# Attention layer: token reordering in two halves, weight splits in another place of the plan, another order of the first loads and projections

## The chip, the cores and the metric

One core of a Trainium2 chip runs the whole program. The metric is the device time of one execution in microseconds (us). The core's engines work side by side, each through its own queue of instructions in a fixed order: TensorE (PE: matmuls and transposes), VectorE (DVE), ScalarE (ACT), GpSimd (POOL), and SyncE (SP), which here only issues the DMA transfers. An instruction that waits holds what stands behind it on its engine.

## The reference

One decoder layer in float32 on x of 1 x 1024 x 1024 (sequence 1024, width 1024): RMS norm, dilated sliding-window attention, added to x; RMS norm, a gated FFN with a short convolution, added to x. Cut to the part that the change touches:

```python
ATTN_GROUPS = ((128, 1), (512, 4), (2048, 16))      # (window, dilation)

def dilated_attention_mixer(h, w_in, q_gain, k_gain, w_out):
    B, S, _ = h.shape
    proj = (h @ w_in).reshape(B, S, 3, 3, 8, 64)      # group, (q, k, v), head, head dim
    outs, lses = [], []
    for g, (window, dilation) in enumerate(ATTN_GROUPS):
        q = rms_norm(proj[:, :, g, 0], q_gain[g]) * 64 ** -0.5
        k = rms_norm(proj[:, :, g, 1], k_gain[g])
        o, lse = dilated_window_attention(q, k, proj[:, :, g, 2], window, dilation)
        outs.append(o); lses.append(lse)
    weights = softmax(stack(lses), axis=0)
    o = sum(weights[..., None] * stack(outs), axis=0)
    return o.reshape(B, S, 512) @ w_out

x = x + dilated_attention_mixer(rms_norm(x, mixer_norm), ...)
x = x + conv_ffn(rms_norm(x, ffn_norm), ...)
```

## The kernel before

**Precision.** Every operand of a matmul is kept as a rounded high part and a low part, the rest. A product is three matmuls: high by high, high by low, low by high. So a weight tile that has arrived is split: ACT casts its high part (L179), and DVE or POOL subtracts to get the low part (L180; DVE for k tiles 0, 2, 4, 5, 7, POOL for 1, 3, 6). Tokens are split in the same way after the transposes that follow the norm (L113; high L115 on ACT, low L116 on DVE) into `hh` and `hl`, which hold the normed x transposed, in eight k tiles of 128 x 1024 with one slot to spare, nine in all.

**Units and blocks.** The attention is done in six units u: the groups in the order 2, 2, 1, 1, 0, 0, each in two halves of four heads. A unit is eight blocks of 128 tokens, 48 blocks in all. Block i projects its tokens (`project`, L198 to L200, into `qk`, and `project_v`, L207 to L209, into `vp`, over eight k tiles each), and then, while PE already projects block i+1, passes through these steps: `norm` (square on ACT, `ss` on DVE, then `ms` and `rs` on POOL, L79 and L80), `values` (`v`, ACT then DVE, L227 and L228), `kept` (POOL makes a part of `kT`), `scale` (`qn`, DVE, L220), `heads_T` (PE transposes to `tr`, L256), `heads_split` (`qT`, `kT`, ACT and DVE), `scores` (`s`, PE, L285), `softmax` (`ust` on DVE, L311; `sm` on ACT, L314), `weights_T` and `weights_split` twice (`pt` on PE, L322; `pT` on ACT and DVE), `attend` twice (`u`, PE), `finish` (DVE, L347) and a write of the block's result to `ud` on SP.

**Weights.** A unit's eight weight tiles are loaded by SP into `raw` (three buffers), split by `load_w` into `w`, a ring of WA = 11. So tiles 0 to 2 of a unit are split far ahead, 3 to 7 in the block before the unit begins, as the old unit's tiles come free.

**Token order.** Each group wants the tokens in another order. Between group 2 and 1 (block 15) and 1 and 0 (block 31) `reorder(g, k)` copies k tile k of `hh` (DVE for even k, ACT for odd) and of `hl` (POOL) into the slot that is free, in the new order; that slot's predecessor becomes free for the next k. A copy of one k is two instructions for g = 1 (L135), four for g = 0 (L142). A copy for k can only run after the last block of the old unit has projected the tile that it overwrites.

**What sets the order.** A list `plan` holds every step with a due time (`at(t, f, ...)`), eight units of time to a block; block i projects k at 8i + k, its v at 8i + 2.6 + 0.85k, and its later steps at 8i + 8 plus an offset from the table `T` (val 0.6, scale 2.5, hT 4.2, sc 6.45, sm 6.5, w0 8.3, a0 12.2, fin 14.4). The steps are written in the order of due times, and PE, ACT, DVE and POOL run them in the order written; the order of SP's DMA issues is made by the scheduler of the tile framework from that order and from what each transfer waits for. `make_masks` (due 90) makes two tables of positions, `kpos`, on POOL, transposes them on PE and makes the masks of groups 1 and 0 on DVE. `tp_gains` loads the gains of q and k and transposes them. `wraw` is a tag of four buffers that x tiles, the first raw tiles, `kpos` and the output weights `w_out` use one after another.

## Time and profile before

| | us |
|---|---|
| median of 3 runs (lowest, highest) | 1334.71 (1334.53, 1338.65) |
| the profiled execution, device time | 1336.1 |
| its span in the trace | 1334.2 |
| PE busy | 1284.2 (96%) |
| DVE busy | 901.2 (68%) |
| ACT busy | 616.0 (46%) |
| POOL busy | 495.9 (37%) |

The page of the profile is read from PE, the busiest engine: a view of the waits names, for PE's idle stretches, the instruction that waited and what released it; the timeline shows instructions of an engine one after another with the idle time before each; the view of stretches gives each engine's busy time, and the granted clock of TensorE as a part of full speed, in a stretch of time that one chooses.

### The profile page before, as it was taken

To read this page: it belongs to the slowest core of one execution; us is meant where nothing else is said; L and a number is where in the kernel's file an instruction comes from. 1 tells how busy PE (TensorE), PEld (TensorE's weight loads), DVE (VectorE), ACT (ScalarE), POOL (GpSimd) and SP (SyncE) were. 2 spreads that over 40 slices of the span, in tenths; PEclk is the share of its full clock that TensorE was granted. 3 is DMA by queue.
4 is the path that set the end of the run, shared out by engine and by line. 5 is a ranking of instruction groups with operands and counts; after the bars stand their busy time and mean duration, and the time that the engine had idled before them with its cause. 6 is when DMAs were issued, how large, how long until landed. Compare 5 with 4: busy or idle time off the path is not lost.

```text
span 1334.2 us, 19243 instructions
## 1 busy us (share of the span) xinstructions
PE 1284.2 (96%) x6911; PEld 1078.4 (81%) x6911; DVE 901.2 (68%) x1544; ACT 616.0 (46%) x1277; POOL 495.9 (37%) x599
## 2 busy tenths in 40 slices
PE   6999998999999999999988999999999999999998
PEld 4898887888878888887766788888888887888887
DVE  4665455454564565556776898888888888876664
ACT  4655354444454444435544444444444536444442
POOL 4333345333354555454533554454454443000000
PEclk9999999999998999999999999999999999999999
DMA  7112212112111121113721333323332328973341
GB/s 240 41 64 75 86 37 72 34 48 61 48 46 35 51 58 50 31 39 122 227 77 39 94 104 111 102 82 100 118 115 83 111 71 283 348 250 105 95 143 64
DMA packets 111614, 132.16 MB, mean 99 GB/s; under 512 B 6126, under 2 KB 80030, under 8 KB 111518
## 3 DMA queue, kind: packets, MB, share of 16 engines
q1 hardware_dynamic: 111518, 130.93, 30.7%
q8 instruction: 55, 0.90, 0.3%
q14 instruction: 41, 0.34, 0.1%
HBM read 95.91 MB, written 35.00 MB: 98 GB/s over the span
## 4 chain that ended last, share of the span: by engine, by line
PE 43%; DVE 3%; issue 2%; DMA 1%; POOL 1%; ACT 1%; SPq 0%; DVEq 0%; POOLq 0%; ACTq 0%
PE ua L687 15%; PE y L871 15%; PE uc L687 8%; PE ub L687 4%; DVE c L732 1%; DMA wB<-in_ffn_w_down 1%; POOL wxl L518 0%; DMA graw<-gde 0%; ACT c L730 0%; DVE sz L660 0%; DVE sy L656 0%; DVE c L743 0%; DVE bt L598 0%; POOL wyl L518 0%; POOL wzl L518 0%
## 5 line engine op out<-in xcount | busy, mean ns | idle before, releaser
L871 PE MATMUL y<-wd,g 128*128 128x512 f32 x924 | 210.4, 389 | 0.2
L871 PEld LDWEIGHTS y<-wd,g 128*128 128x128 f32 x924 | 173.4, 188 | 36.9 <-DVE wd L598 0.6
L198 PE MATMUL qk<-w,hh 128*128 128x512 f32 x384 | 159.0, 414 | 0.5 <-ACT hh L115 0.5
L199 PE MATMUL qk<-w,hh 128*128 128x512 f32 x384 | 153.5, 400 | 0.0
L200 PE MATMUL qk<-w,hl 128*128 128x512 f32 x384 | 152.6, 397 | 0.5 <-DVE hl L116 0.5
L79 POOL TENSOR_SCALAR ms<-ss 128x8 f32<-128x8 f32 (+1 forms) x64 | 12.9, 201 | 312.9 <-DVE ss L216 265.9
L207 PE MATMUL vp<-w,hh 128*128 128x256 f32 x384 | 122.8, 320 | 3.6 <-DVE v L228 3.6
L732 DVE SCALAR_TENSOR_TENSOR c<-uu,cw,c 128x1023 f32<-128x1023 f32 (+1 forms) x44 | 95.6, 2174 | 38.3 <-ACT c L730 37.5
L209 PE MATMUL vp<-w,hl 128*128 128x256 f32 x384 | 108.8, 283 | 0.0
L208 PE MATMUL vp<-w,hh 128*128 128x256 f32 x384 | 108.8, 283 | 0.0
L518 POOL TENSOR_TENSOR wyl<-sy,wyh 128x1024 fp32r<-128x1024 f32 x21 | 56.5, 2689 | 115.0 <-issue 61.0
L80 POOL TENSOR_TENSOR rs<-ms,half 128x8 f32<-128x8 f32 (+1 forms) x64 | 87.5, 1367 | 5.4
L207 PEld LDWEIGHTS vp<-w,hh 128*128 128x128 f32 x384 | 73.5, 192 | 18.5 <-DVE v L228 5.8
L314 ACT ACTIVATE sm<-sm,ust 128x128 f32<-128x128 f32 (+1 forms) x128 | 53.4, 418 | 76.0 <-DVE ust L311 73.4
L200 PEld LDWEIGHTS qk<-w,hl 128*128 128x128 f32 x384 | 73.3, 191 | 18.7 <-DVE hl L116 1.2
L267 ACT ACTIVATE qT<-tr,gains 128x256 fp32r<-128x256 f32 x48 | 22.7, 473 | 134.8 <-PE tr L256 134.8
L216 DVE TENSOR_REDUCE ss<-qn 128x8 f32<-128x512 f32 x48 | 32.9, 685 | 75.8 <-ACT qn L214 75.8
L208 PEld LDWEIGHTS vp<-w,hh 128*128 128x128 f32 x384 | 73.6, 192 | 9.3
L270 DVE SCALAR_TENSOR_TENSOR qT<-tr,gains,qT 128x256 fp32r<-128x256 f32 x48 | 23.2, 484 | 85.5 <-ACT kT L269 85.5
L518 POOL TENSOR_TENSOR wxl<-uraw,wxh 128x1024 fp32r<-128x1024 f32 x22 | 58.4, 2653 | 44.8 <-ACT wxh L517 44.7
L198 PEld LDWEIGHTS qk<-w,hh 128*128 128x128 f32 x384 | 74.0, 193 | 1.1 <-ACT hh L115 0.9
L199 PEld LDWEIGHTS qk<-w,hh 128*128 128x128 f32 x384 | 74.1, 193 | 0.1
(186 smaller groups left out, 3363.0 us busy)
## 6 DMA issues: line engine op xcount, KB each, us to landing
uraw<-in_ffn_w_up SPq DMA_DIRECT2D x44, 512.0 KB
raw<-in_attn_w_in SPq DMA_DIRECT2D x48, 384.0 KB
wB<-in_ffn_w_down SPq DMA_DIRECT2D x44, 256.0 KB
graw<-gds SPq DMA_DIRECT2D x44, 256.0 KB
gdo<-c SPq DMA_DIRECT2D x11, 512.0 KB
gds<-gbc SPq DMA_DIRECT2D x11, 512.0 KB
graw<-gdo SPq DMA_DIRECT2D x22, 256.0 KB
ud<-ust SPq DMA_DIRECT2D x32, 132.0 KB
```

The lines of the kernel that those rows point to most:

```text
L80: nc.gpsimd.tensor_tensor(r[:, :n], t[:, :n], half[:, :n], op=ALU.pow)
L198: nc.tensor.matmul(self.qk, a, w[:, 0, :512], start=k == 0, stop=False)
L199: nc.tensor.matmul(self.qk, a, w[:, 1, :512], start=False, stop=False)
L200: nc.tensor.matmul(self.qk, b, w[:, 0, :512], start=False, stop=k == KT - 1)
L207: nc.tensor.matmul(self.vp, a, w[:, 0, 512:], start=k == 0, stop=False)
L208: nc.tensor.matmul(self.vp, a, w[:, 1, 512:], start=False, stop=False)
L209: nc.tensor.matmul(self.vp, b, w[:, 0, 512:], start=False, stop=k == KT - 1)
L314: nc.scalar.activation(sm[:, h, lo:], sm[:, h, lo:], AF.Exp, scale=-1.0, bias=st[:, 256 + h:257 + h], accum_out=st[:, 260 + h:261 + h])
L518: eng.tensor_sub(l, raw, h.bitcast(F32))
L687: nc.tensor.matmul(acc[:, lo:hi], w[z][:, s + k], a[y][:, j, k, lo:hi], start=begin and lo == 0 and k == 0 and n == 0, stop=k == 3 and n == 2,
L732: nc.vector.scalar_tensor_tensor(c[:, k:], u[:, :S - k], cw[:, 2 - k, j:j + 1], c[:, k:], op0=ALU.mult, op1=ALU.add)
L871: nc.tensor.matmul(y, gs[:, z, ts], ws[:, w], start=f and n == 0, stop=k == NK - 1 and n == 2, skip_group_check=True)
```

## The change

Five edits, all in the attention part:

- **The first loads and block 0.** SP issues x of chunk 0, the gain row `gbc`, raw tiles 0 to 4, x of chunk 1, raw tiles 5 to 7; before, raw tile 0 came ahead of `gbc`, and x of chunk 1 behind raw tile 2. DVE scales chunk 0 ahead of the first weight split. Chunk 1 is scaled behind four of DVE's five splits of unit 0, before behind two (counting the one ahead of chunk 0); its transposes were due at 0.5 and 0.6 and are due at 5.5 and 5.7, between the v projections of k tiles 3 and 4 of block 0. The loads of the q and k gains have a step of their own (2.5), and their transposes are due at 8.3.
- **The masks.** POOL's part, `kpos`, becomes `mask_places`, due at 76.8; PE's and DVE's part stays in `make_masks`, due at 86.5.
- **The reordering.** `reorder` takes the half (h or l), the k tile and the copying engine. The low half's k = 0 to 4 are copied by POOL from 28 units ahead of the block before the change of group, one every five units, into `hl`'s free slot and, for group 1, four further tiles `hx` (tag `wraw`); group 0 reads these and writes back to `hl`. The low k = 5 to 7 follow in the block itself. The high half's k = 0 is copied on ACT 4.4 units ahead of that block; k = 1 to 7 follow in it at offsets given by a table, odd k on ACT, even k on DVE.
- **The weight splits.** Tiles 3 to 7 of a new unit were due 3.1 to 7.1 units into the block before it. Now tile 3 is due at 3.9, and 4 to 7 at 8.7, 9.45, 10.6 and 12.6 where u is even, at 5.4, 8.7, 9.6 and 10.8 where u is odd; `values` of that block is at 8.6. The issue of raw tiles 6 and 7 goes with the splits of 3 and 4.
- **What follows for SP.** Since `hx` and the output weights share the tag `wraw`, `w_out`'s loads wait for `hx`'s last readers in block 31; before, they followed `kpos`.

```diff
@@ -117,29 +118,37 @@
 
 
 
-    slot0 = {2: 0, 1: 8, 0: 7}
-
-    def toks(g, t, k, c):
-
-        return t[:, (k + slot0[g]) % (KT + 1), c * P:(c + 1) * P]
-
-    def reorder(g, k):
-
-        for t, copy in ((hh, nc.scalar.copy if k % 2 else nc.vector.tensor_copy), (hl, nc.gpsimd.tensor_copy)):
-            src, dst = (t[:, (k + slot0[x]) % (KT + 1)] for x in (g + 1, g))
-            if g == 1:
-
-                src = src.rearrange("p (e r b n) -> p e r b n", e=2, r=4, b=2)
-                dst = dst.rearrange("p (r b e n) -> p e r b n", e=2, r=4, b=2)
+    places = {("h", 2): [*range(8)], ("h", 1): [8, *range(7)], ("h", 0): [7, 8, *range(6)],
+              ("l", 2): [*range(8)], ("l", 1): [8, "a", "b", "c", "d", 0, 1, 2],
+              ("l", 0): [3, 4, 5, 6, 7, 8, 0, 1]}
+    extra = {}
+
+    def place(z, g, k):
+        s = places[z, g][k]
+        return extra[s] if isinstance(s, str) else (hh if z == "h" else hl)[:, s]
+
+    def toks(g, z, k, c):
+
+        return place(z, g, k)[:, c * P:(c + 1) * P]
+
+    def reorder(g, z, k, copy):
+
+        if isinstance(places[z, g][k], str):
+            extra[places[z, g][k]] = A.tile([P, S], F32R, name="hx", tag="wraw", bufs=4)
+        src, dst = place(z, g + 1, k), place(z, g, k)
+        if g == 1:
+
+            src = src.rearrange("p (e r b n) -> p e r b n", e=2, r=4, b=2)
+            dst = dst.rearrange("p (r b e n) -> p e r b n", e=2, r=4, b=2)
+            for e in range(2):
+                copy(dst[:, e], src[:, e])
+        else:
+
+            src = src.rearrange("p (r b e c n) -> p b c e r n", r=4, b=2, e=2, c=4)
+            dst = dst.rearrange("p (b c e r n) -> p b c e r n", r=4, b=2, e=2, c=4)
+            for b in range(2):
                 for e in range(2):
-                    copy(dst[:, e], src[:, e])
-            else:
-
-                src = src.rearrange("p (r b e c n) -> p b c e r n", r=4, b=2, e=2, c=4)
-                dst = dst.rearrange("p (b c e r n) -> p b c e r n", r=4, b=2, e=2, c=4)
-                for b in range(2):
-                    for e in range(2):
-                        copy(dst[:, b, :, e], src[:, b, :, e])
+                    copy(dst[:, b, :, e], src[:, b, :, e])
 
     def rows(g, t, c):
 
...
@@ -193,7 +202,7 @@
 
             if k == 0:
                 self.qk = PQ.tile([P, 512], F32, name="qk", bufs=2)
-            a, b = toks(self.g, hh, k, self.c), toks(self.g, hl, k, self.c)
+            a, b = toks(self.g, "h", k, self.c), toks(self.g, "l", k, self.c)
             w = Ws[self.u, k]
             nc.tensor.matmul(self.qk, a, w[:, 0, :512], start=k == 0, stop=False)
             nc.tensor.matmul(self.qk, a, w[:, 1, :512], start=False, stop=False)
@@ -202,7 +211,7 @@
         def project_v(self, k):
             if k == 0:
                 self.vp = PA.tile([P, 256], F32, name="vp", bufs=1)
-            a, b = toks(self.g, hh, k, self.c), toks(self.g, hl, k, self.c)
+            a, b = toks(self.g, "h", k, self.c), toks(self.g, "l", k, self.c)
             w = Ws[self.u, k]
             nc.tensor.matmul(self.vp, a, w[:, 0, 512:], start=k == 0, stop=False)
             nc.tensor.matmul(self.vp, a, w[:, 1, 512:], start=False, stop=False)
@@ -409,57 +418,77 @@
     def first(i):
         xs[i] = Normed(i, xs[i])
 
-    def tp_gains():
-        grow = A.tile([P, 4, P], F32, name="grow", tag="qn", bufs=2)[:6, 0]
+    gr = {}
+
+    def load_gains():
+        gr[0] = grow = A.tile([P, 4, P], F32, name="grow", tag="qn", bufs=2)[:6, 0]
         for t in range(2):
             nc.sync.dma_start(grow[0:3, t * DH:(t + 1) * DH], q_gain)
             nc.sync.dma_start(grow[3:6, t * DH:(t + 1) * DH], k_gain)
+
+    def tp_gains():
+        grow = gr[0]
         tp = PA.tile([P, 512], F32, name="tp", tag="tr", bufs=2)
         nc.tensor.transpose(tp[:, :6], grow, ident[:6, :6])
         nc.vector.tensor_scalar(gains[:, 0:3], tp[:, 0:3], DH ** -0.5, None, op0=ALU.mult)
         nc.vector.tensor_copy(gains[:, 3:6], tp[:, 3:6])
 
-    def make_masks():
-        places = A.tile([P, 8, P], F32, name="kpos", tag="wraw", bufs=4)
-        kpos, kint = places[:, 0:2], places[:, 2:4].bitcast(I32)
+    kp = {}
+
+    def mask_places():
+        t = A.tile([P, 8, P], F32, name="kpos", tag="wraw", bufs=4)
+        kp[0] = kpos = t[:, 0:2]
+        kint = t[:, 2:4].bitcast(I32)
         nc.gpsimd.iota(kint[:, 0], pattern=[[1, 8], [8, 16]], base=0, channel_multiplier=0)
         nc.gpsimd.iota(kint[:, 1], pattern=[[1, 2], [2, 64]], base=0, channel_multiplier=0)
         nc.gpsimd.tensor_copy(kpos, kint)
-        kp = PA.tile([P, 4, P], F32, name="kp", tag="tr", bufs=2)
+
+    def make_masks():
+        kpos = kp[0]
+        t = PA.tile([P, 4, P], F32, name="kp", tag="tr", bufs=2)
         for g in range(2):
-            nc.tensor.transpose(kp[:, g], kpos[:, g], ident)
-        nc.vector.tensor_copy(qpos, kp[:, 0:2, 0])
+            nc.tensor.transpose(t[:, g], kpos[:, g], ident)
+        nc.vector.tensor_copy(qpos, t[:, 0:2, 0])
         for g in range(2):
             for j, beyond in enumerate((ALU.is_lt, ALU.is_gt)):
                 nc.vector.tensor_scalar(mask[:, g, j], kpos[:, g], qpos[:, g:g + 1], NEG, op0=beyond,
                                         op1=ALU.mult)
 
     blocks = [Block(u, n) for u in range(6) for n in range(8)]
-    early = [(-20, -19.6, -19.35, -18), (-19.1, -17.8, -17.65, .5)]
+    early = [(-20, -19.2, -19.15, -18.9), (-19.3, -18.4, -18.2, 5.5)]
     for i in range(8):
         t = early[i] if i < 2 else (8 * i - 12, 8 * i + T["xf"], 8 * i + T["xs"], 8 * i + T["xt"])
         at(t[0], get_x, i)
         at(t[1], first, i)
         at(t[2], lambda i: xs[i].scale(), i)
         at(t[3], lambda i: xs[i].turn(0), i)
-        at(t[3] + .1, lambda i: xs[i].turn(1), i)
-    at(-19.4, get_gain)
-    at(2.5, tp_gains)
-    at(90, make_masks)
+        at(t[3] + .2, lambda i: xs[i].turn(1), i)
+    at(-19.9, get_gain)
+    at(2.5, load_gains)
+    at(8.3, tp_gains)
+    at(76.8, mask_places)
+    at(86.5, make_masks)
     for g, i in ((1, 16), (0, 32)):
-        for k in range(KT):
-            at(8 * (i - 1) + T["vs"] * (k - 1) + T["v"] + .02, reorder, g, k)
+        t = 8 * (i - 1)
+        at(t - 4.4, reorder, g, "h", 0, nc.scalar.copy)
+        for k in range(5):
+            at(t - 28 + 5 * k, reorder, g, "l", k, nc.gpsimd.tensor_copy)
+        for k, d in enumerate((2.62, 3.47, 4.6, 5.3, 6.1, 7.3, 8.65), 1):
+            at(t + d, reorder, g, "h", k, nc.scalar.copy if k % 2 else nc.vector.tensor_copy)
+        for k, d in enumerate((3.5, 5.3, 7.0) if g == 1 else (3.5, 7.2, 9), 5):
+            at(t + d, reorder, g, "l", k, nc.gpsimd.tensor_copy)
     SP = WA - KT
     for u in range(6):
         wt = {}
         for kt in range(KT):
             if u == 0:
-                t = lead = (-19.5, -19.3, -19.2)[kt] if kt < 3 else -18 + .1 * kt
+                t = (-19.1, -19, -18.8, -18.6, -18.5, -18.3, -18.1, -18)[kt]
+                lead = -19.8 + .1 * kt if kt < 5 else -18.7 + .05 * kt
             elif kt < SP:
                 t = 64 * u - 32 + T["wp"] + 4 * kt
                 lead = t - 3
             else:
-                t = 64 * u - KT + max((kt - SP) * T["vs"] + T["v"] + .01, kt - SP + T["w"])
+                t = 64 * u - KT + (3.9, *((8.7, 9.45, 10.6, 12.6) if u % 2 == 0 else (5.4, 8.7, 9.6, 10.8)))[kt - SP]
                 lead = max(t - 8, 64 * u - KT + (kt - SP - 3) * 1. + T["w"] + .5) if kt < SP + 3 else wt[kt - 3] + .3
             wt[kt] = t
             at(lead, load_raw, u, kt)
```

What stands on the engines is shown at three places. PE at the start: transposes `xT` of a chunk of x, then block 0's projections (`qk`, `vp`), three matmuls to a k tile. Before, from the first instruction on:

```order
L113 MATMUL xT<-ident,xn 128x128 x8
L198 MATMUL qk<-w,hh 128x512
L199 MATMUL qk<-w,hh 128x512
L200 MATMUL qk<-w,hl 128x512
L113 MATMUL xT<-ident,xn 128x128 x8
L198 MATMUL qk<-w,hh 128x512
L199 MATMUL qk<-w,hh 128x512
L200 MATMUL qk<-w,hl 128x512
```

and now, behind the first transposes, five k tiles of `qk` and three of `vp`:

```order
L207 MATMUL qk<-w,hh 128x512
L208 MATMUL qk<-w,hh 128x512
L209 MATMUL qk<-w,hl 128x512
L216 MATMUL vp<-w,hh 128x256
L217 MATMUL vp<-w,hh 128x256
L218 MATMUL vp<-w,hl 128x256
L114 MATMUL xT<-ident,xn 128x128 x8
L216 MATMUL vp<-w,hh 128x256
L217 MATMUL vp<-w,hh 128x256
L218 MATMUL vp<-w,hl 128x256
L207 MATMUL qk<-w,hh 128x512
```

The second set of transposes stood behind the first k tile of `qk`; now it stands behind six of `qk` and four of `vp`.

DVE in the first part of block 15, the last of group 2 (`qn` from `qk` is the scaling, `hh<-hh` a high copy, `w<-raw` a weight split, `ust<-u` is `finish`). Before:

```order
L329 TENSOR_TENSOR pT<-pt,pT 128x256
L135 COPY hh<-hh 128x8x64 x2
L220 TENSOR_TENSOR qn<-qk,rs 128x512
L135 COPY hh<-hh 128x8x64 x2
L329 TENSOR_TENSOR pT<-pt,pT 128x256
L180 TENSOR_TENSOR w<-raw,w 128x768
L270 SCALAR_TENSOR_TENSOR qT<-tr,gains,qT 128x256
L273 SCALAR_TENSOR_TENSOR kT<-tr,gains,kT 64x2x128 x2
L180 TENSOR_TENSOR w<-raw,w 128x768
L135 COPY hh<-hh 128x8x64 x2
L347 TENSOR_REDUCE ust<-u 128x256
L135 COPY hh<-hh 128x8x64 x2
```

and now:

```order
L338 TENSOR_TENSOR pT<-pt,pT 128x256
L229 TENSOR_TENSOR qn<-qk,rs 128x512
L144 COPY hh<-hh 128x8x64 x2
L338 TENSOR_TENSOR pT<-pt,pT 128x256
L279 SCALAR_TENSOR_TENSOR qT<-tr,gains,qT 128x256
L282 SCALAR_TENSOR_TENSOR kT<-tr,gains,kT 64x2x128 x2
L144 COPY hh<-hh 128x8x64 x2
L356 TENSOR_REDUCE ust<-u 128x256
```

Four copies and two splits stood there, two copies stand there now.

DVE at the end of block 15 (`ss` belongs to `norm`, `v` to `values`). Before:

```order
L180 TENSOR_TENSOR w<-raw,w 128x768
L216 TENSOR_REDUCE ss_2303<-qn 128x8
L228 TENSOR_TENSOR v<-vp,v 128x4x64
L329 TENSOR_TENSOR pT<-pt,pT 128x256
L220 TENSOR_TENSOR qn<-qk,rs 128x512
L329 TENSOR_TENSOR pT<-pt,pT 128x256
L270 SCALAR_TENSOR_TENSOR qT<-tr,gains,qT 128x256
L273 SCALAR_TENSOR_TENSOR kT<-tr,gains,kT 64x2x128 x2
```

and now:

```order
L144 COPY hh<-hh 128x8x64 x2
L225 TENSOR_REDUCE ss_2291<-qn 128x8
L237 TENSOR_TENSOR v<-vp,v 128x4x64
L189 TENSOR_TENSOR w<-raw,w 128x768
L338 TENSOR_TENSOR pT<-pt,pT 128x256
L189 TENSOR_TENSOR w<-raw,w 128x768
L229 TENSOR_TENSOR qn<-qk,rs 128x512
L338 TENSOR_TENSOR pT<-pt,pT 128x256
L279 SCALAR_TENSOR_TENSOR qT<-tr,gains,qT 128x256
L282 SCALAR_TENSOR_TENSOR kT<-tr,gains,kT 64x2x128 x2
L189 TENSOR_TENSOR w<-raw,w 128x768
```

One split stood ahead of `ss`; now one copy stands there, two splits stand between `v` and the scaling, and one behind `kT`.

## Rows read from the trace of the kernel before

**Rows 1.** Page, part 1: busy time, share of the span, instructions.

```profile
PE 1284.2 (96%) x6911; PEld 1078.4 (81%) x6911; DVE 901.2 (68%) x1544; ACT 616.0 (46%) x1277; POOL 495.9 (37%) x599
```

**Rows 2.** PE's waits, 0 to 560 us: total us, times, longest us.

```profile
PE xT L113 <- DVE xn L107: 11.9, 2, 9.0
PE pt L322 <- ACT sm L314: 6.1, 2, 3.1
PE vp L207 <- DVE v L228: 3.6, 5, 1.1
PE kp L430 <- POOL kpos L427: 3.0, 1, 3.0
PE tr L256 <- DVE qn L220: 2.3, 2, 1.8
...
PE qk L198 <- ACT hh L115: 0.5, 1, 0.5
...
PE s L285 <- POOL kT L245: 0.3, 1, 0.3
```

**Rows 3.** Timeline of PE, start: start us, length us, instruction, [idle before <- releaser].

```profile
11.49 0.80 PE L198 MATMUL qk<-w,hh 128*128 128x512 f32 x1 [0.55 <-ACT hh L115]
...
16.90 1.94 PE L113 MATMUL xT<-ident,xn 128*128 128x128 f32 x8 [2.89 <-DVE xn L107]
...
20.77 0.63 PE L200 MATMUL qk<-w,hl 128*128 128x512 f32 x1
...
28.73 0.40 PE L198 MATMUL qk<-w,hh 128*128 128x512 f32 x1
```

**Rows 4.** Timelines of DVE and ACT, start.

```profile
7.64 1.28 DVE L107 SCALAR_TENSOR_TENSOR xn<-xt,rs,gbc 128x1024 f32<-128x1024 f32 x1
...
13.92 2.83 DVE L107 SCALAR_TENSOR_TENSOR xn<-xt,rs,gbc 128x1024 f32<-128x1024 f32 x1 [0.17 <-POOL rs L80]
...
17.00 0.83 ACT L179 CAST w<-raw 128x768 fp32r<-128x768 f32 x1 [0.23 <-DMA raw<-in_attn_w_in]
```

**Rows 5.** Timelines of POOL and DVE about the masks.

```profile
144.50 1.64 POOL L80 TENSOR_TENSOR rs<-ms,half 128x8 f32<-128x8 f32 x1
...
147.81 0.88 DVE L434 TENSOR_SCALAR mask<-kpos,qpos 128x128 f32<-128x128 f32 x4
```

**Rows 6.** Stretches: length; busy PE, PEld, DVE, ACT, POOL; clock, DMA, GB/s.

```profile
148.00:151.40 3.40, 3.40 (x12) 2.93 (x11) 1.62 (x6) 0.13 (x1) 0.12 (x1) 0.50 0.29 89
...
410.80:414.20 3.40, 3.40 (x15) 3.14 (x14) 1.57 (x3) 0.29 (x1) 0.00 (x0) 0.51 0.00 0
```

**Rows 7.** PE's waits, 195 to 215 us (blocks 15 and 16).

```profile
PE pt L322 <- ACT sm L314: 3.1, 1, 3.1
PE s L285 <- DVE kT L273: 1.0, 1, 1.0
PE vp L207 <- DVE v L228: 0.8, 1, 0.8
PE tr L256 <- DVE qn L220: 0.6, 1, 0.6
```

**Rows 8.** Timelines of DVE, POOL and ACT about block 15.

```profile
193.03 0.76 DVE L135 CAST hh<-hh 128x512 fp32r<-128x512 f32 x2
194.57 0.69 DVE L220 TENSOR_TENSOR qn<-qk,rs 128x512 f32<-128x512 f32 x1 [0.78 <-POOL rs L80]
195.18 1.51 DVE L135 CAST hh<-hh 128x512 fp32r<-128x512 f32 x2
...
200.57 0.96 DVE L180 TENSOR_TENSOR w<-raw,w 128x768 fp32r<-128x768 f32 x1
...
213.69 0.69 DVE L220 TENSOR_TENSOR qn<-qk,rs 128x512 f32<-128x512 f32 x1 [2.28 <-POOL rs L80]
...
200.85 5.94 POOL L135 CAST hl<-hl 128x512 fp32r<-128x512 f32 x8
...
203.12 1.14 ACT L135 CAST hh<-hh 128x512 fp32r<-128x512 f32 x2 [3.13 <-DVE hh L135]
```

## The prediction

> **What bounds the kernel now.** I read the page first: TensorE (PE) is busy for 96% of the span [rows 1], so it is the bound, and a change can gain only where PE stands still or runs slowly, or lose by making it stand. Next, PE's waits up to 560 us, in which the whole attention lies [rows 2, 7]: the reader is to see that they add up to some 29 us, and nearly all lie in five kinds of place. At the start PE waits 11.9 us in two goes for the normed x (`xT <- xn`) and 0.5 us each for the first high and the first low part (two rows, one shown). At 147 us it waits 3.0 us for `kpos`, which GpSimd (POOL) makes for the masks. At the five unit ends it waits 3.6 us for `v`. The other waits (`pt <- sm`, `tr <- qn`, `s <- kT`) lie where one token order is turned into the next, in blocks 15 and 31. For the first of these I asked the same view of 195 to 215 us alone [rows 7]: 1.0 + 3.1 + 0.8 + 0.6 = 5.5 us. Third, the granted clock: in four stretches of 3.4 us, at 148, 206, 400.6 and 410.8 us, each just behind such a wait, PE had 0.50 or 0.51 of its clock, so 1.2 instead of 2.4 GHz (the first and the last stand in [rows 6]); at the higher level the work in one would have taken half the time, so each costs 1.7 us. The start has a stretch like it: a 128x512 matmul takes 0.63 us at 20.8 us and 0.40 us at 28.7 us [rows 3].
>
> **Start.** Two edits act. The first split of block 0's weights (0.96 us) no longer runs on VectorE (DVE) ahead of `xn` of chunk 0, which starts at 7.64 us now [rows 4]; it can start at about 6.85, when its row scale is there. That moves the first projection from 11.49 us [rows 3] to about 10.5. The larger: after three matmuls PE now turns to chunk 1's transposes and waits for its `xn`, and block 0's other projections stand behind them. After the change six weight tiles of block 0 come first and the transposes behind v of tile 3. So PE works from 10.5 us on, and the 11.8 us of PE work that lie between the second transposes at 16.9 us and block 1's second projection at 28.73 us [rows 3] follow the first three matmuls (1.3 us): 10.5 + 1.3 + 11.8 = 23.6 us. Half clock is in that figure, since PE runs its first 5 us at it either way. Against it stand arrivals: the last raw tile lands at 17.0 us now [rows 4], and the same bytes are asked for in nearly the same order. ACT's cast (0.83 us) and DVE's split (0.96) follow, and `xn` of chunk 1 stands ahead of that split on DVE: 1.28 us alone, 2.83 beside POOL [rows 4]. So the last low part is there between 19.2 and 20.7 us, with about 2 us of PE work behind it, and block 1's second projection comes between 22.6 and 25.2 us. I take 24.0: a gain of 4.7 us (3.5 to 6.1). The q and k scales' transposes cost their 0.1 us in either place; their loads, issued earlier, have 3 us more to land.
>
> **Masks.** `kpos` was late because its instructions stood behind a 1.64 us `rs` on POOL [rows 5]. They move to a gap of POOL 13 of the plan's units earlier (eight are a block), and PE's two transposes find them ready. That removes 3.0 us and, with the gap, the half clock behind it: 4.7 us. The DVE part (0.88 us for four instructions [rows 5], and a smaller one) now runs in a steady block, ahead of `sm`, where PE has some slack; I charge 0.5. Gain 4.2 us (3.5 to 4.7).
>
> **Waits for v.** Of 3.6 us, 0.8 belong to block 15 [rows 7]. The other 2.8, at the ends of units 0, 2, 4 and in block 31, come from two or three splits of the next unit that stand on ACT and DVE ahead of `v`. At the odd units' starts one of five is left ahead, and the rest goes behind `v`, where one split of 0.96 us fits in DVE's gap. All 2.8 go (1.4 to 2.8).
>
> **Reordering at block 15.** Here DVE did four high copies of 1.5 us beside POOL (0.76 alone), and splits, ahead of `kT`, `sm` and `v`; ACT waited 3.13 us in its row for one of DVE's; POOL copied for 5.94 us in one go, which made `kT`, `ms` and `rs` late [rows 8]. After the change five of eight low copies are done 5 to 28 units earlier, in POOL's idle time; one high copy goes to ACT before the stage; two splits go from before `sm` to behind `v`. That leaves on DVE one copy of 1.5 us in each of three places. The 3.1 us before `pt` go: ahead of `sm` stand one copy and `ust` instead of two copies, `ust`, a split and the waits between. What becomes late next: `tr` of block 15. Between `ss` and the scaling of `qn` DVE has 2.28 us in which it waits for POOL's `rs` [rows 8]. Into it now go two splits. ACT must first do v, a 1.14 us copy and a 0.83 us cast, so that the first split can start some 1.4 us after v; with 0.96 + 0.41 (`pT`) + 0.96 behind it, scaling comes 3.7 us after v, where PE's own work from v to `tr` is 2.7. I charge 1.2 us for it, 1.4 for three short waits (`pt`, `vp`, `u`) behind copies of 1.5 us on DVE and 1.14 on ACT, and 0.3 for a chance of half clock: 2.9 left of 5.5 + 1.7 = 7.2. Gain 4.3 us. The bounds: 7.2 if nothing is late, 2 if the short waits stay as they were.
>
> **Reordering at block 31.** The same sum: by rows 2 less rows 7, 3.0 (`pt`) + 1.7 (`tr`) + 0.3 (`s`) = 5.0 us (its v is counted above), and two half-clock stretches, 3.4: 8.4. Block 31 scores two tiles of keys, so PE has more work of its own between the same steps, and I leave only `tr` behind the two splits, 1.3 us. Gain 7.1 us (5 to 8.4).
>
> **What else moves, at nothing.** The early low copies, ten of about 1.5 us each (5.94 for four [rows 8]), go to POOL, busy for 37% of the span [rows 1]. They lengthen DVE work that runs beside them: the one high copy was 1.51 instead of 0.76 us, but scaling of `qn` beside POOL's copies took its usual 0.69 [rows 8], and most of DVE's work in a steady block is of this kind, reading PSUM. If each of ten cost PE 0.3 us, it would be 3 us; I take zero. On SP, w_out's four loads now need the extra tiles' last reader in block 31 and stand there between two raw tiles of unit 4; the tile behind them is needed by ACT some 6 us after it can land. The raw tile of kt 7 is issued only after kt 4's split; from the start, where eight such tiles and more landed in 17 us [rows 4], I estimate that it lands within some 2 us, about one before it is cast. Cover gone, each microsecond would be one of PE.
>
> By the rows a DVE copy beside POOL costs 1.51 us instead of 0.76 [rows 8], and that is what I used. The Trainium skill (SBUF — State Buffer, section "Who interferes with whom") says more: who issues first has the ports shared by DVE and GpSimd for its whole instruction, and the other is blocked. Before, POOL's copies were short ones; after, one of DVE's copies in block 15 meets POOL's split of a whole weight tile. By that rule it would wait for all of it, an estimated 1 us more in `sm`, and the sum would be 22 instead of 23 us.
>
> **Sum.** 4.7 + 4.2 + 2.8 + 4.3 + 7.1 = 23.1 us. PE's row count is the same, and all behind the attention (out-projection, FFN, down-projection) is untouched and waits for PE, so the gain passes through. The profiled execution took 1336.1 us with a span of 1334.2; less 23.1 that is 1313.0. It lies 1.4 us above the median of the runs, 1334.71, from which 1311.6 follows. I say 1311.5.
>
> **Rivals.** First, *the splits behind v become the new wait*. At the two even boundaries scaling waits longer than I sum, PE stands for 2.5 to 3 us, and the clock halves behind it. For: the row with 2.28 us has no room for two splits and their casts; before, one `tr` wait of 1.7 was followed by half clock [rows 6]. Against: PE's own work covers 2.7 of it. Each place 3 to 4.5 us: 1316 to 1325, likeliest 1319. Second, *all waits go*: copies and splits overlap better than by rows; then 29 us are gained, 1305.5. Third, *slower*: a single mechanism, SP's queue at the even boundaries. SP issues in order; a raw tile that waits for a split which waits for the ring's slot holds w_out and the `ud` writes behind it, and PE waits for weights. It decides from about 3 us later than summed; to be slower than before it has to cost 11.5 us at each of two places beyond that, and over 13 to be measurably so: 1339. Against: the same estimate of 2 us for a landing, and a DMA share of 0.00 in the stretch just behind block 31's waits [rows 6]. Fourth, *it doesn't do what it says*: the order is on the engines, but arrivals set the start and the copies just shift their lateness; within 4 us of before, 1333.
>
> **How the numbers follow.** The forecast 0.63, own range 1306 to 1316; splits as a new wait 0.20; all gone 0.11; slower 0.03; no effect 0.03. The range takes in the forecast, most of the first rival and the edge of the second: 1305.5 to 1320. A measurement here tells about 0.3%, 4 us, from no change. Faster 0.94, same 0.03, slower 0.03.
>
> **What would show it.** Start: block 1's second projection at 24 us, and no `xT` wait but the first, at 8.2. Masks: no `kp` wait, clock 1.00 behind it. v: no `vp` waits at odd units. Boundaries: no `pt` wait over 1 us, a `tr` wait of 1 to 1.5, clock near 1. Wrong would be a `tr`, `s` or `qk` wait of over 2 us there, a second half-clock stretch, or PE waiting for a raw tile.

## The result, and the profile after

The changed kernel takes 1315.38 us (median of four runs, 1313.31 to 1317.68) against 1335.76 for the kernel before on the same chips: a ratio of 0.9845, 95% interval 0.9821 to 0.9869, so 20.4 us less (17.5 to 23.9). The forecast was 1311.5, 23.2 us less than the median of before known then, in a range of 1305.5 to 1320. The profiled execution went from 1336.1 to 1315.75 us, its span from 1334.2 to 1313.7.

PE's waits up to 560 us in the changed kernel, the view of [rows 2, 7] (total us, times, longest us):

```profile
PE xT L114 <- DVE xn L108: 8.6, 2, 8.4
PE tr L265 <- DVE qn L229: 3.0, 5, 0.9
PE qk L208 <- POOL w L189: 0.6, 1, 0.6
PE qk L208 <- DVE w L189: 0.4, 2, 0.3
PE pt L331 <- ACT sm L323: 0.3, 1, 0.3
```

29 us of waiting have become 13. `kp` and both long waits for `sm` are gone, and with them the half clock that followed: the stretches that answer to [rows 6], behind the masks, block 15 and block 31 (two), now run at the full 2.4 GHz (stretch; busy PE, PEld, DVE, ACT, POOL; granted clock; DMA share; GB/s):

```profile
138.00:141.40 3.40, 3.40 (x21) 2.65 (x20) 1.35 (x3) 1.58 (x6) 1.69 (x2) 1.00 0.00 0
...
193.00:196.40 3.40, 3.25 (x18) 2.51 (x18) 1.19 (x4) 3.38 (x11) 1.31 (x2) 1.00 0.00 1
...
382.00:385.40 3.40, 3.40 (x21) 2.75 (x20) 1.52 (x3) 3.38 (x10) 1.86 (x3) 1.00 0.72 280
392.00:395.40 3.40, 3.40 (x28) 2.95 (x25) 2.19 (x10) 2.21 (x9) 0.00 (x0) 1.00 0.50 146
```

Five waits for `qn` stand where there were two, one at each of the five unit changes. One of them, and the start, on PE's timeline (start us, length us, instruction, idle before and its releaser):

```profile
10.43 0.79 PE L207 MATMUL qk<-w,hh 128*128 128x512 f32 x1
11.02 0.63 PE L208 MATMUL qk<-w,hh 128*128 128x512 f32 x1
11.44 0.57 PE L209 MATMUL qk<-w,hl 128*128 128x512 f32 x1
11.86 0.40 PE L207 MATMUL qk<-w,hh 128*128 128x512 f32 x1
...
14.63 0.50 PE L208 MATMUL qk<-w,hh 128*128 128x512 f32 x1 [0.63 <-POOL w L189]
...
18.46 1.06 PE L114 MATMUL xT<-ident,xn 128*128 128x128 f32 x8 [0.19 <-DVE xn L108]
...
23.45 0.40 PE L207 MATMUL qk<-w,hh 128*128 128x512 f32 x1
...
199.07 0.66 PE L265 MATMUL tr<-ident,qn 128*128 128x128 f32 x4 [0.70 <-DVE qn L229]
```

**A ledger by place.** PE runs the same instructions in nearly the same order in both kernels, so the start of the same projection can be read in both timelines and subtracted. Here it is the second projection (k = 1) of a block; a block's row runs from there to the next block's second projection.

| stretch | forecast us | changed kernel us | where |
|---|---|---|---|
| to block 1 | 4.7 | 5.3 (28.73 to 23.45) | start |
| blocks 10 and 11 | 4.2 | 4.5 | masks |
| blocks 8, 24, 40 | 2.8 with block 31's `v` | 0.1 | `v` at the odd units' starts |
| blocks 15 to 17 | 4.3 | 5.1 | first reordering |
| blocks 31 to 33 | 7.1 | 8.3 | second reordering |
| all, up to block 47 | 23.1 | 23.1 (591.78 to 568.65) | the attention |
| behind block 47 | 0 | -2.9 | out-projection, FFN, down-projection |

The sum over the attention came out to the tenth, though one of its terms did not, and 2.9 us were lost where nothing was changed. From one execution to the next a block's row moves by less than 0.1 us unless a half-clock stretch comes or goes; the start moves more, without an edit: in five executions with the old order block 1's second projection came at 28.1 to 29.5 us, in nine with the new one at 23.1 to 24.3.

### The profile page after: what moved, and what is told of

It is laid out like the page before. It is cut to its first block, busy times and chain, and to the rows that moved or that the text cites. A ratio compares the mean times of both kernels' runs of the same rounds, so it can differ in the third digit from the quotient of the medians.

```text
span 1313.7 us, 19221 instructions
## 1 busy us (share of the span) xinstructions
PE 1280.4 (97%) x6911; PEld 1075.1 (82%) x6911; DVE 896.7 (68%) x1538; ACT 617.3 (47%) x1283; POOL 494.5 (38%) x599
## 4 chain that ended last, share of the span: by engine, by line
PE 45%; DVE 2%; issue 1%; POOL 1%; ACT 1%; DMA 1%; SPq 0%; ACTq 0%; POOLq 0%; DVEq 0%
PE ua L716 17%; PE y L900 15%; PE uc L716 9%; PE ub L716 4%; DVE c L761 1%; DMA graw<-gde 0%; POOL wxl L547 0%; ACT c L759 0%; DMA wB<-in_ffn_w_down 0%; DVE sz L689 0%; DVE bt L627 0%; POOL wyl L547 0%; POOL wzl L547 0%; DVE x L586 0%; DVE sy L685 0%
## 5 line engine op out<-in xcount | busy, mean ns | idle before, releaser
L209 PE MATMUL qk<-w,hl 128*128 128x512 f32 x320 | 125.6, 393 | 0.0
L218 PE MATMUL vp<-w,hl 128*128 128x256 f32 x320 | 90.0, 281 | 0.0
L279 DVE SCALAR_TENSOR_TENSOR qT<-tr,gains,qT 128x256 fp32r<-128x256 f32 x48 | 23.2, 483 | 82.4 <-ACT kT L278 82.4
L320 DVE CUSTOM_DVE_ANT_0 sm<-s,mask 128x128 f32<-128x128 f32 (+1 forms) x192 | 56.1, 348 | 24.0 <-PE s L298 18.5
```

The lines of the kernel that those rows point to most:

```text
L209: nc.tensor.matmul(self.qk, b, w[:, 0, :512], start=False, stop=k == KT - 1)
L218: nc.tensor.matmul(self.vp, b, w[:, 0, 512:], start=False, stop=k == KT - 1)
L320: nc.vector.tensor_tensor_reduce(out=sm[:, h, lo:], in0=src[h], in1=m, op0=ALU.add, op1=ALU.min, scale=-1.0, scalar=3e38, accum_out=st[:, ...
```

## The experiments

### Each part alone

Four kernels, each the kernel before with one part. The start:

```diff
-    early = [(-20, -19.6, -19.35, -18), (-19.1, -17.8, -17.65, .5)]
+    early = [(-20, -19.2, -19.15, -18.9), (-19.3, -18.4, -18.2, 5.5)]
...
-                t = lead = (-19.5, -19.3, -19.2)[kt] if kt < 3 else -18 + .1 * kt
+                t = (-19.1, -19, -18.8, -18.6, -18.5, -18.3, -18.1, -18)[kt]
+                lead = -19.8 + .1 * kt if kt < 5 else -18.7 + .05 * kt
```

(with `load_gains`, `tp_gains` and `get_gain` as in the changed kernel.)

> The kernel before with the start alone changed (order of the first loads, block 0 projected as weights arrive, gains behind it). If the parts add up, block 1's second projection comes at 23.4 us instead of 28.7 and the attention ends 5.3 us earlier; every later wait of the kernel before stays: kp 3.0, pt 3.1 and 3.0, tr 2.3, five v waits 3.6. Total about 1330. Rival: the gain at the start is given back at the first unit change, because later loads come no earlier; then the attention ends less than 3 us earlier.

Measured: 1330.53 us against 1336.31 on the same chip. Block 1's second projection 5.5 us earlier, and the attention's end 5.5 us earlier: nothing is given back on the way.

The masks:

```diff
-    at(90, make_masks)
+    at(76.8, mask_places)
+    at(86.5, make_masks)
```

> The kernel before with the masks alone changed (kpos made 13 units earlier, masks ahead of where they stood). If the parts add up: no kp wait, no half clock at 148 us, the attention ends 4.5 us earlier (3.0 of waiting, 1.7 of clock, less 0.2 for DVE's mask instructions). Rival: the half clock belongs to that stretch and not to the wait; then it stays at 148 us and only 2.8 us are gained.

Measured: 1331.38 us; blocks 10 and 11 take 4.5 us less, no `kp` wait, no half clock there. So the half clock went with the wait. But the wait does not always bring it: the reordering alone (below) still has the 3.0 us wait for `kpos`, no half clock behind it in its execution, and gains 1.6 us there without an edit. So one such stretch cost 1.6 us here, in the same block and behind the same wait (1.7 in the prediction).

The reordering alone is the changed kernel with the start, the masks and this line taken back; the splits alone is the kernel before with this line changed:

```diff
-                t = 64 * u - KT + max((kt - SP) * T["vs"] + T["v"] + .01, kt - SP + T["w"])
+                t = 64 * u - KT + (3.9, *((8.7, 9.45, 10.6, 12.6) if u % 2 == 0 else (5.4, 8.7, 9.6, 10.8)))[kt - SP]
```

> The kernel before with the reordering alone changed (low half ahead, high half on the new offsets), the weight splits where they were. Theory: the copies were the greater part of the two boundary stalls, so 8 to 10 of the 13.4 us that the two boundaries gained come back (4.6 to 5 at block 15, 4 to 5 at block 31), and the v waits at the odd units stay (1.1, 0.7, 0.4). Rival: copies and splits each fill DVE and ACT alone, so that either left in place keeps most of the stall; then under 5 us together.

> The kernel before with the weight splits alone moved behind the values, the reordering as before. Theory: 2 to 5 us less at the two boundaries (the copies still stand ahead of kT and sm) and 0.1 to 0.2 at the odd units together, as in the changed kernel, where rs on POOL was lengthened. Rival: the splits were the stall; then over 8 us of the 13.4, and the odd units' 2.2 us of v waits come back as well, because rs is lengthened only beside early copies.

Measured: 1330.01 and 1330.40 us. At the two changes of group:

| | blocks 15 to 17 | blocks 31 to 33 |
|---|---|---|
| reordering alone | 2.3 | 3.0 |
| splits alone | 1.1 | 4.0 |
| both (changed kernel) | 5.1 | 8.3 |

My theory that the copies were the greater part (8 to 10 us) is wrong, and so is that the splits were. Each alone leaves a long wait in place. PE's waits from 190 to 215 us, the reordering alone:

```profile
PE pt L331 <- ACT sm L323: 2.3, 1, 2.3
PE vp L216 <- DVE v L237: 0.8, 1, 0.8
PE s L294 <- DVE kT L282: 0.2, 1, 0.2
```

and the splits alone:

```profile
PE pt L322 <- ACT sm L314: 2.6, 1, 2.6
PE vp L207 <- DVE v L228: 1.2, 1, 1.2
PE s L285 <- DVE kT L273: 1.0, 1, 1.0
```

Before it was 3.1 for `pt` [rows 7]; with both parts 0.3 (the last line of the first view above). At block 31 the reordering alone leaves 2.5 us for `v` and 1.4 for `sm`, the splits alone 3.1 for `sm`. Copies and splits fill the same queues ahead of the same steps, and either is enough to keep a stall. Part of these gains is clock: of the half-clock stretches that before had at 206, 401 and 411 us, the reordering alone keeps two (204 and 402 us), the splits alone one (399), the changed kernel none. At the 1.6 us measured above for one, an estimate, the waits and delays themselves are 8.6 us of the 13.4 together, 3.7 and 2.0 alone: the parts still need each other. A caution on block 31's figures: the kernel before, run once more (below), needed 1.5 us less in blocks 31 to 33 than its first profile, because the second of the two half-clock stretches there did not come. Against that execution the three rows read 1.5, 2.5 and 6.8.

The splits alone gained 0.1 us in all at the odd units, as in the changed kernel: the missing 2.2 us there have nothing to do with the early copies.

### Why the odd units gained nothing

At the start of unit 1 (block 8) the `v` wait of the kernel before is gone, and a wait of 0.4 us for `qn`, with smaller gaps, stands for it. DVE, POOL and PE there in the changed kernel:

```profile
105.87 0.96 DVE L189 TENSOR_TENSOR w<-raw,w 128x768 fp32r<-128x768 f32 x1
...
108.36 0.69 DVE L229 TENSOR_TENSOR qn<-qk,rs 128x512 f32<-128x512 f32 x1 [1.20 <-POOL rs L80]
108.97 1.96 DVE L189 TENSOR_TENSOR w<-raw,w 128x768 fp32r<-128x768 f32 x1
...
105.93 2.40 POOL L80 TENSOR_TENSOR rs<-ms,half 128x8 f32<-128x8 f32 x1
108.30 1.81 POOL L189 TENSOR_TENSOR w<-raw,w 128x768 fp32r<-128x768 f32 x1
...
109.11 0.55 PE L265 MATMUL tr<-ident,qn 128*128 128x128 f32 x3 [0.44 <-DVE qn L229]
```

DVE is not the late one: it stands idle 1.20 us for `rs`. The moved split starts 0.06 us ahead of `rs`, and `rs` takes 2.40 us instead of 1.64 [rows 5]. At unit 3 it is 2.40 again. At unit 5 `rs` starts 0.07 us ahead of the split and takes 1.64, but there another pair meets: POOL's split of tile 6 starts 0.13 us ahead of a tiny DVE instruction of the merge, `e`, 128x12, which takes 0.17 us elsewhere:

```profile
482.97 0.96 DVE L189 TENSOR_TENSOR w<-raw,w 128x768 fp32r<-128x768 f32 x1
...
484.64 1.72 DVE L372 TENSOR_TENSOR e<-nm,mt 128x12 f32<-128x12 f32 x1
486.28 0.68 DVE L229 TENSOR_TENSOR qn<-qk,rs 128x512 f32<-128x512 f32 x1
...
482.90 1.64 POOL L80 TENSOR_TENSOR rs<-ms,half 128x8 f32<-128x8 f32 x1
484.51 1.83 POOL L189 TENSOR_TENSOR w<-raw,w 128x768 fp32r<-128x768 f32 x1
```

To measure the collision by itself I put one instruction behind `v` in quiet blocks:

```diff
+        scr = hl[:, 7, :768]
+        if kind[0] == "two":
+            nc.vector.tensor_sub(scr, a, b)
+        elif kind[0] == "copy":
+            nc.vector.tensor_copy(scr, a)
+        else:
+            nc.vector.tensor_reduce(small.tile([P, 8], F32, name="ss8"), a.rearrange("p (h d) -> p h d", d=96), axis=AX.X, op=ALU.add)
```

> The changed kernel with one more VectorE instruction right behind v in five quiet blocks, its output unused: in blocks 18 and 26 a subtraction of two SBUF tiles 128x768 (0.96 us, the same as a weight split), in 20 and 28 a copy of one such tile, in 22 a sum over one. Theory: a split that starts just ahead of rs on POOL lengthens it; rs then takes 2.3 to 2.5 us instead of 1.64 in blocks 18 and 26 and tr waits 0.3 to 0.6 us there, and in 22 (one input, no fast mode) rs stays 1.64 and nothing waits; the copy lies between. Rival: at the odd units scaling was late because DVE was occupied or because of something else at a unit's end; then rs stays 1.64 in all five.

`rs` in blocks 18, 20 and 22, with the added DVE instruction ahead of it:

```profile
229.76 0.95 DVE L410 TENSOR_TENSOR hl<-w 128x768 fp32r<-128x768 f32 x1
...
229.96 2.25 POOL L80 TENSOR_TENSOR rs<-ms,half 128x8 f32<-128x8 f32 x1
...
253.21 0.55 DVE L412 CAST hl<-w 128x768 fp32r<-128x768 f32 x1
...
253.33 1.92 POOL L80 TENSOR_TENSOR rs<-ms,half 128x8 f32<-128x8 f32 x1
...
276.66 0.94 DVE L414 TENSOR_REDUCE ss<-w 128x8 f32<-128x768 f32 x1
...
276.86 1.64 POOL L80 TENSOR_TENSOR rs<-ms,half 128x8 f32<-128x8 f32 x1
```

Blocks 26 and 28 repeat the first two (2.25 and 1.93 us). A subtraction of two SBUF tiles lengthens `rs` by 0.61 us, the copy by 0.28, a sum as long as the subtraction not at all: occupied time on DVE is not it. The second half of the expectation missed: no `tr` wait appeared, and the attention ended within 0.1 us of where it did (the total, 1317.17 us, differs behind it). In these five blocks of the changed kernel the transposes begin 1.1 us after scaling has ended; in blocks 7 and 23 of the kernel before, whose steps run at the starts of units 1 and 3, they began 0.2 us after it. So a lengthened `rs` costs PE only where that slack is small.

How much longer can be read from the rows: about what the earlier instruction still has to run, less 0.14 us. At block 8 the split still had 0.90 us when `rs` started, and `rs` took 0.76 more; the added subtraction had 0.75 and cost 0.61, the copy 0.43 and 0.28; POOL's split had 1.70 when `e` started, which took 1.55 more, and 1.14 when DVE's split started at 108.97, which took 1.00 more. One order is harmless: a DVE split that starts after `rs`, as at 482.97, takes its usual time. All thirteen in the changed kernel's attention that start while such an `rs` runs take 0.96 to 0.98.

The Trainium skill, in the section that the prediction quoted (SBUF — State Buffer, section "Who interferes with whom"), says that a DVE instruction with two SBUF inputs contends with a GpSimd instruction that reads SBUF, that the one that issues first holds the ports for its whole instruction, and that a reduction does not contend. The added subtraction and sum, and `e`, agree with it; the splits behind `rs` do not, since `rs` held up none of them.

### The splits out of the gap

If the splits between `v` and the scaling are what `tr` waits for, they should go elsewhere. DVE has 1.7 us of idle time between `sm` and `ss`, if the cast on ACT has been done ahead of `sm`. So cast and subtraction got due times of their own:

```diff
-... ((8.7, 9.45, 10.6, 12.6) if u % 2 == 0 else (5.4, 8.7, 9.6, 10.8)))[kt - SP]
+... ((7.45, 9.45, 10.6, 12.6) if u % 2 == 0 else (5.4, 7.0, 9.6, 12.0)))[kt - SP]
...
-            at(t, load_w, u, kt)
+            cast = {(1, 5): 6.2, (0, 4): 5.9}.get((u % 2, kt)) if u else None
+            at(t if cast is None else 64 * u - KT + cast, load_w, u, kt)
+            at(t, load_low, u, kt)
```

> The changed kernel with one split per unit moved off the stretch between v and the scaling: at odd units tile 5 is cast ahead of sm and subtracted between sm and ss, tile 7 goes behind the second pT; at even units the same for tile 4 (cast ahead of the fifth copy). If these splits are what tr waits for: rs 1.64 us and no tr wait at the odd units (0.4 to 0.9 us gained at each of three), tr waits at blocks 15 and 31 of 0.7 and 0.9 gone, the attention ends 2 to 4 us earlier than in the changed kernel. Rival: ss or v become late behind the moved split, and vp waits take the place; then within 0.7 us of the changed kernel.

Measured: 1310.94 us. The attention ends 1.9 us earlier than in the changed kernel, just under what was expected; four of the five `tr` waits are gone. At units 1 and 3 the gain (0.9 and 0.5) was lost in the block ahead of it (0.9 and 0.4): 7.0 is also the due time of `sm` there, and the subtraction came out ahead of `sm` by the tie. With 7.1 instead:

> The run with the moved splits, with tile 5's subtraction at the odd units due 7.1 instead of 7.0, so that it stands behind sm on VectorE and not, by a tie of due times, ahead of it. Theory: block 7 keeps its 10.9 us (11.8 in that run) and block 23 its 12.0 (12.4), the odd units' gain of 0.9 and 0.5 us stays, the attention ends 3.2 us earlier than in the changed kernel, and the total lies at 1309 to 1313. Rival: ss behind the moved split is late and vp waits instead; then no better than the run before.

```profile
PE xT L114 <- DVE xn L108: 8.4, 1, 8.4
PE vp L219 <- DVE v L240: 0.5, 3, 0.2
PE tr L268 <- DVE qn L232: 0.3, 1, 0.3
PE pt L334 <- ACT sm L326: 0.3, 1, 0.3
```

Measured: 1308.85 us, median of five runs (1308.77 to 1310.51), against 1337.6 for the kernel before on that chip: ratio 0.9789, interval 0.9776 to 0.9802, so better than both kernels, and just below the span of the expectation. The ledger against the changed kernel, part by part: 0.9 us at each of blocks 8, 16 and 24, 0.7 at block 40, 0.3 at blocks 32 and 33, and 0.3 at the start, which was not touched: 4.0 us, 3.7 of them the moved splits'. The two profiles are 6.9 us apart; the other 2.9 lie behind the attention (next section). At block 8 `rs` is back at its length:

```profile
105.60 1.64 POOL L80 TENSOR_TENSOR rs<-ms,half 128x8 f32<-128x8 f32 x1
```

### The 2.9 us behind the attention

From block 47's second projection to the last matmul PE runs the same code in all kernels, and its longest waits are the same everywhere (2.7 us for `xn`, 1.8 for `wxl`, 2.1 and 1.3 at a `uc`). All its idle time there is 16.8 us in the first profile of before and 16.0 in that of after. Yet it took 738.1 us in the first profile of before and 741.1 in that of after. What differs is the clock. The changed kernel behind three such waits, where the two stretches that answer to the first two ran at 1.00 in the kernel before:

```profile
646.20:649.60 3.40, 3.40 (x14) 2.73 (x13) 3.14 (x6) 0.69 (x2) 0.00 (x0) 0.57 0.38 153
674.00:677.40 3.40, 3.40 (x9) 2.66 (x8) 2.29 (x4) 1.63 (x2) 0.00 (x0) 0.50 0.00 0
708.20:714.80 6.60, 5.08 (x12) 4.01 (x13) 4.55 (x4) 1.91 (x3) 1.72 (x2) 0.50 0.11 42
```

```profile
669.00:673.00 4.00, 4.00 (x23) 3.39 (x22) 3.29 (x7) 1.38 (x3) 0.00 (x0) 1.00 0.32 132
697.00:701.00 4.00, 4.00 (x19) 3.33 (x18) 2.43 (x3) 2.09 (x3) 0.00 (x0) 1.00 0.02 4
```

Is that the kernel, its place in time, or the execution? The changed kernel twice more, the kernel before once more, and the changed kernel with more PE work in block 45, its result written over:

```diff
+            for _ in range(2 if (self.u, self.c, k) == (5, 5, 0) else 0):
+                nc.tensor.matmul(self.qk, a, w[:, 0, :512], start=True, stop=False)
+                nc.tensor.matmul(self.qk, a, w[:, 1, :512], start=False, stop=False)
+                nc.tensor.matmul(self.qk, b, w[:, 0, :512], start=False, stop=True)
```

> The changed kernel as it is, another execution. Question: the 2.9 us given back behind the attention. If the extra half-clock stretches there (five, the kernel before two) come from the kernel's order, they stand again at the same places, and 1315 to 1316 comes again. If they vary from execution to execution, their number changes and the time goes with it, about 1 us for each; the attention itself ends within 0.3 us of the first profile.

> As the run before it: the changed kernel once more, for the number and the places of the half-clock stretches behind the attention.

> The changed kernel with six more matmuls of 128x512 in block 45 (a projection step done twice more, its result written over), 1.4 us of PE work, so that everything behind the attention begins 1.4 us later and is otherwise the same. Theory: which of the waits behind the attention is followed by half clock hangs on when they fall; then the set of stretches (585, 646, 674, 708 us) changes and the total moves by something other than 1.4 us, by up to 2 or 3 either way. Rival: the set belongs to the waits; then the same four places 1.4 us later and 1.4 us more in total.

> As the run before it with twelve more matmuls, 2.8 us of PE work. Theory: another set of half-clock stretches again, the total not 2.8 us more than the changed kernel's. Rival: the same set, 2.8 us more.

> The kernel before as it is, another execution. If the set of half-clock stretches belongs to a kernel, it has two behind the attention again, at 609 and 731 us, and the attention ends where it did; if it varies from execution to execution, other places.

| kernel | total us | block 47 to the last matmul, us | half-clock stretches there, us |
|---|---|---|---|
| before | 1336.10 | 738.1 | 609, 731 |
| before, again | 1337.35 | 740.4 | 606 to 620, 671, 732 |
| after | 1315.75 | 741.1 | 585, 646, 674, 708 to 715 |
| after, again | 1314.57 | 740.2 | 584, 646, 673, 710 |
| after, again | 1315.54 | 741.1 | 585, 646, 674, 708 to 714 |
| 1.4 us more work | 1316.83 | 740.9 | 586, 647, 675, 709 to 715 |
| 2.8 us more work | 1321.67 | 743.4 | 587 to 601, 652, 680, 714 to 720 |
| five more DVE instructions | 1317.17 | 742.4 | 645, 662 to 669, 676, 713 |
| splits out of the gap (7.1) | 1308.85 | 738.2 | 581, 642, 704 |

(Those without a length are 3 to 4 us long, and places are within 1 us. The other five traces have 738.2 to 739.4 us there: each part alone, and the first run with moved splits.) 1.4 us more work left the set as it was, against my theory; 2.8 us more lengthened the first stretch to 13.5 us, and the total moved by more than the work, against its rival (0.9 us of it at the start, which varies by itself). In the kernel before two executions of one program differ by 2.3 us in this part, with a 13.5 us stretch in one at which the other had 3.4:

```profile
606.50:620.00 13.50, 12.96 (x51) 10.61 (x50) 10.31 (x25) 5.56 (x14) 6.92 (x12) 0.50 0.20 77
```

So the part behind the attention takes 738 to 743 us, and its waits don't order the runs: idle time is 14.4 us in before, again, and 16.8 in before. What is left without the idle time goes with the time at 1.2 GHz in all 14 traces: 721 us with 7 us of half clock, 722 to 723 with 10, 724 with 14, 725 to 726 with 17, 726 with 20.5, 728.5 with 27. The four executions behind the median of after show the same in total: 1313.31 us at a mean granted clock of 0.996, 1315.01 and 1315.75 at 0.993, 1317.68 at 0.989. The 2.9 us are this part's clock, not a transfer or a wait that the change made; between the means of the two executions of before and the three of after it is 1.5 us. What decides whether a wait is followed by a slow stretch, and how long it is, these runs don't settle, nor whether the changed kernel's order has a part in it.

The Trainium skill (TensorE: Matmul & The Clock Gate, Part 1) says of a kernel's first matmuls that the gate's monitor runs on its own time, so that one kernel can show different numbers of slow ones in different runs. The two executions of the kernel before differ in the same way, in the middle of the kernel; no run here tests more of it.

## Why the prediction was right

Four of five terms had the right mechanism, and the time lies in the range. That the attention's sum came out at 23.1 us is luck: start, masks and the two changes of group gave 0.6, 0.3, 0.8 and 0.6 us more than forecast, `v` at the odd units 2.1 less.

- **Start.** Right in mechanism, 5.3 instead of 4.7 us. The first projection came at 10.43 us (forecast 10.5). Two errors partly cancelled: I counted half clock for PE's first 5 us as before; it lasted three matmuls behind the transposes (0.79, 0.63, 0.57 us, then 0.40). Against that PE waited 0.63 us for POOL's split of tile 3, which the sum did not name, and less for others. The last low part came at 20.8 us, just past the forecast's 19.2 to 20.7, and was hidden.
- **Masks.** 4.5 against 4.2. The charge of 0.5 for DVE's mask instructions ahead of `sm` was too high. They made `v` 0.5 us late in block 11, of which PE lost 0.2 (11.1 us against 10.85 in its neighbours). Block 10 takes 0.2 us more too, but that is PE's own two transposes, which stood in block 11 before.
- **Waits for v.** The step that failed: "one split of 0.96 us fits in DVE's gap". It did fit on DVE, but the gap is the time of POOL's `rs`, and at units 1 and 3 the split lengthened that, at unit 5 a POOL split held up a DVE instruction. 0.1 us came of the 2.2 at the odd units; with the splits elsewhere 2.5 more came. The rule that I had quoted for one copy in block 15 applied here (with the exception above), to instructions for which I had used the undisturbed rows.
- **Block 15.** 5.1 against 4.3. The `tr` wait behind two splits came as argued: DVE waited 1.01 us for ACT's cast behind its copy, and scaled after the second split; it cost 0.70 us, I had 1.2. The three short waits, 1.4 in the sum, are 0.3. Block 17 takes 0.4 us more than before, which the sum had not; it does in the splits alone too, and not in the reordering alone. The collision of a DVE copy with POOL's split, by the Trainium skill's rule an estimated 1 us, did not happen: POOL's split ended 0.07 us ahead of the copy, and the copies that ran beside POOL's copies took 1.05 and 1.51 us. No half clock.
- **Block 31.** 8.3 against 7.1 and block 31's `v` (0.6 of the 2.8). `tr` waits 0.92 us (forecast 1.3). Some 1.5 us of the 8.3 is a half-clock stretch that the kernel before has in one execution and not in another.
- **Behind the attention.** "The gain passes through" failed by 2.9 us between the two profiles. The waits there did pass nearly unchanged; the clock behind them did not. I had seen that a wait costs its length and a half-clock stretch, counted the stretches of the attention as lost with their waits, and did not put the same uncertainty on the waits that stay.
- **The rivals.** The splits behind `v` did become the new wait, at all five unit changes, but with 3.0 us in all instead of 3 to 4.5 at each of two, and without half clock. SP's queue cost PE nothing, but not for the reason given. The raw tile of kt 7 was to land within 2 us, one ahead of its cast; at block 31 SP issued it at 385.88, and ACT stood for it until 390.39, 4.5 us later:

```profile
390.39 0.84 ACT L188 CAST w<-raw 128x768 fp32r<-128x768 f32 x1 [0.94 <-DMA raw<-in_attn_w_in]
```

Its low part was ready at 392.22, 0.8 us before PE read it. PE's one wait for a weight there, 0.3 us, was for DVE's split of another tile.

## What to carry to other kernels

When two kinds of work fill the queues ahead of one stalled step, moving either alone shows little: both together gave 13.4 us here, alone 5.3 and 5.2, of which some 5, 2 and 3 are half-clock stretches that went. A gap on one engine that is the running time of an instruction on another is not free for work that collides with it: look which of the two starts first, and what the earlier one has left to run. Here a split 0.06 us ahead of `rs` cost 0.76 us, one 0.07 us behind it nothing. And where waits are followed by a slower clock, part of a gain made early can be lost, or more can be won, behind waits that nobody touched; a ledger by place, from the same instruction in both traces, tells that apart from a wrong sum.

## What the runs showed that I had not expected

- A DVE instruction on 128x12 took 1.72 us instead of 0.17, because POOL's 1.83 us split had started 0.13 us ahead of it; with the moved splits it runs 0.9 us ahead of that split, and took 0.17 again.
- `rs` on 128x8 takes 1.64 us, 2.25 to 2.40 with a 0.96 us DVE subtraction started just ahead of it, and 1.64 with the same subtraction started 0.07 us behind it, which then takes its 0.96 as well.
- A half-clock stretch of 13.5 us behind waits of 1.1 us and less (before, again, at 606 us), where another execution of the same program had 3.4 us.
